# The gate of the input embedding by seven products of blocks, five of them mixed with the first row tiles of the up projection

## The chip, the cores and the metric

One core of one Trainium2 chip runs the whole layer. Its engines are TensorE (PE, matmuls, with weight loads listed as PEld), VectorE (DVE), ScalarE (ACT), GpSimd (POOL) and SyncE (SP, which issues most DMAs). The metric is the device time of one execution in microseconds (us), lower is better.

## The reference, cut to what matters

A decoder layer over 512 tokens of width 1024 in float32. The part that matters here stands between the two layer norms; h, p, w_pe and w_pe_gate have the shapes 512x1024, 512x256, 256x1024 and 1024x1024, and the up projection is 1024 wide in and 2 x 2816 wide out.

```python
h = _layer_norm(DN_ALPHA * h + mixed @ w_o[i], ln1_g[i], ln1_b[i]).astype(dt)
up = _causal_dwconv(h @ w_up[i], conv_w[i], conv_b[i])
val, gate = up[..., :D_FF], up[..., D_FF:]
ffn = (jax.nn.silu(gate) * val) @ w_down[i]
ple = (p[i].astype(dt) @ w_pe[i]) * jax.nn.sigmoid(h @ w_pe_gate[i])
h = _layer_norm(DN_ALPHA * h + ffn + ple, ln2_g[i], ln2_b[i]).astype(dt)
```

## The kernel before

Every float32 product is made of three products of rounded parts: an operand is split into a high part (ACT, a cast) and a low part (DVE, a subtraction), and `mm3` (L274) adds high x high, high x low and low x high. A matmul has a weight tile of 128x128 and 512 columns. Weights come in pages of 128x1024: `Weights` loads a page on SP's queue (L104) and splits it (L121, L122), some pages ahead of their use.

Pages are tiles of 4 KB a partition out of one pool; a page that is freed goes to the end of the list (`Pages`, L45), and its next user waits for its last reader. When the state-space part is through, `more_pages` (L1451) adds 14.

`mid` (L1103) does, in this order: the output projection of row tiles 0 and 1 (four banks, 8 k); their norms; the same for tiles 2 and 3, in which the transposes of tiles 0 and 1 are written behind k = 3 and k = 5 (`trans`, L1132: 8 transposes on PE, then 8 splits of 128x128 from PSUM into the pages hT); the norms of tiles 2 and 3; the embedding p @ w_pe of each tile (`pe`, L1121); then the gate of each tile (`gate`, L1145: 2 halves x 8 k x 3 matmuls, a sigmoid, a multiplication with the embedding, and ALPHA x row + product), with the transposes of tiles 2 and 3 behind the gates of 0 and 1. A norm is two statistics and an aggregate on DVE, 9 steps of one column on POOL for the root (`rsqrt`, L1045), and two wide steps on DVE (L1030, L1031).

`ffn_up` (L1201) follows. For each of 22 feature tiles f and each half (value, gate) it runs 24 matmuls over hT, then the convolution: one step on ACT (L1215) and two on DVE (L1216, L1217); a Silu, and for f under 16 `combine` (L1234), which makes the operands of the down projection. For that one, `Products` (L172) already takes seven products of blocks in place of eight: its pages are loaded, negated on ACT (L208) and added to another block by an accumulating DMA that POOL issues (L209). From f = 16 on these products alternate with the up projection.

The framework orders the instructions of each engine by its own simulation of their readiness. Only where `in_order` is set (L264) does each matmul stay behind the one written before it: in the attention stage and from f = 16 on, but not in `mid`.

Of the kernel before, what the change touches and what calls it, by code (L numbers as in the profile page):

```python
# [30 lines left out]
NPAGES_LATE = 14  # L31
# [140 lines left out]
class Products:  # L172
# [5 lines left out]
    ORDER = (("11", None, 0),  # L178
             ("22", None, "12"),
             ("-T3", 1, "11"),  # L180
             ("T2", 2, "21"),
             ("11", 0, "12"),
             ("21", None, 0),
             ("22", None, 0))
    KEPT = (0, 1, 2)

    def __init__(self, tc, pages, blocks, fetch_ahead=5, split_ahead=1):
        self.nc, self.pages, self.blocks = tc.nc, pages, blocks
        self.fa, self.sa = fetch_ahead, split_ahead
        self.per = NS // 2  # L190
        self.raw, self.hl = {}, {}
        self.nf = self.ns = 0
        self.n = len(self.ORDER) * self.per

# [3 lines left out]
    def fetch_to(self, n):  # L198
        while self.nf < min(n, self.n):
            q, j = divmod(self.nf, self.per)  # L200
            name, of, plus = self.ORDER[q]
            if of is None:
# [7 lines left out]
            self.raw[q, j] = pg  # L210
            self.nf += 1

    def split_to(self, n):
        while self.ns < min(n, self.n):
            self.fetch_to(self.ns + 1)
            q, j = divmod(self.ns, self.per)
            raw = self.raw[q, j]
# [4 lines left out]
            if q not in self.KEPT:  # L222
                self.raw.pop((q, j)).free()
# [8 lines left out]
    def free(self, n):  # L232
        for pg in self.hl.pop(n):
            pg.free()


class Layer:
    def __init__(self, tc, cst, pages, banks, a):
# [16 lines left out]
        self.wpg = add("w_pe_gate")  # L255
# [3 lines left out]
        self.WP = Products(tc, pages, a["w_down_blocks"])  # L259


    def mm(self, out, lhsT, rhs, start, stop):
        ins = self.nc.tensor.matmul(out=out, lhsT=lhsT, rhs=rhs, start=start, stop=stop, skip_group_check=True).ins  # L263
        if self.in_order:  # L264

# [837 lines left out]
    def mid(self):  # L1103
        nc, W = self.nc, self.W
        ple = []
# [15 lines left out]
        def pe(t):  # L1121
            ws = [W.use(self.wpe + k) for k in range(2)]
            pg = self.pages.get(f"ple{t}")
            for h in range(2):
# [3 lines left out]
                nc.scalar.copy(pg.t[:, h * 512:h * 512 + 512], bank.t)  # L1128
                bank.free()
            ple.append(pg)  # L1130
# [411 lines left out]
```

## Time and profile before

| | us |
|---|---|
| median of three runs | 794.27 |
| these runs | 796.55, 791.86, 794.27 |
| the profiled execution | 791.56 |
| its span, first to last instruction | 789.9 |
| PE busy in it | 774.6 |
| DVE busy | 546.0 |
| ACT busy | 365.9 |

The span is a little under the time of the execution it belongs to. Busy time of an engine is the time in which at least one of its instructions runs, so overlapping matmuls count once. The stage of `mid` is the stretch from 330.9 to 432.5 us; the up projection begins there and ends among the down products near 716.

### The profile page before, as it was taken

How to read it: one execution, taken by the hardware profiler on the slowest of the kernel's cores; microseconds unless marked ns; L12 is line 12 of the kernel's file. 1: busy time of each engine (PE TensorE's matmuls, PEld its weight loads, DVE VectorE, ACT ScalarE, POOL GpSimd, SP SyncE). 2: the span in 40 equal slices, each digit the busy share in tenths (PEclk: the TensorE clock that was granted, in tenths of full speed). 3: DMA queues.
4: the chain of work that ended last, by engine and by line, in shares of the span. 5: the costliest groups of instructions: out<-in, count | busy, mean ns of one | idle time of the engine just before them, and what ended most of it. 6: DMA issues, size and time to landing. Idle time of an engine off the chain costs nothing.

```text
span 789.9 us, 9826 instructions
## 1 busy us (share of the span) xinstructions
PE 774.6 (98%) x3668; PEld 647.7 (82%) x3668; DVE 546.0 (69%) x960; ACT 365.9 (46%) x578; POOL 34.7 (4%) x74
## 2 busy tenths in 40 slices
PE   9999999999999999999999999999999999999996
PEld 7888888878888888888888888888888878888885
DVE  6967998697666968947753675665755576778456
ACT  6435667664343356514522344343444676556300
POOL 0000000000000000005300000000001211000000
PEclk9999999999999999999999999999999999999998
DMA  8913221024112547515212352013325986428102
GB/s 315 391 72 101 60 74 61 27 85 132 51 54 69 182 151 293 168 46 172 96 54 79 108 191 77 0 54 107 134 100 116 256 194 137 104 84 278 39 27 81
DMA packets 32176, 95.14 MB, mean 120 GB/s; under 512 B 4480, under 2 KB 8704, under 8 KB 31872
## 3 DMA queue, kind: packets, MB, share of 16 engines
q1 hardware_dynamic: 29248, 85.07, 31.7%
q0 software_dynamic: 2304, 8.39, 5.8%
q10 hardware_dynamic: 576, 1.05, 0.4%
q8 instruction: 29, 0.48, 0.2%
q14 instruction: 19, 0.16, 0.1%
HBM read 88.20 MB, written 3.15 MB: 116 GB/s over the span
## 4 chain that ended last, share of the span: by engine, by line
PE 90%; DVE 3%; ACT 2%; DMA 2%; issue 1%; SPq 0%; DVEq 0%; ACTq 0%
PE up L263 28%; PE g L263 10%; PE o L263 6%; PE pg L263 6%; PE mx L263 6%; PE X L263 5%; PE z L263 4%; PE Y L263 4%; PE V L263 4%; PE u L263 3%; PE A L263 3%; PE v L263 3%; PE kb L263 2%; PE qb L263 2%; DMA dr<-in_w_down_blocks_dram 2%; PE pe L263 1%
## 5 line engine op out<-in xcount | busy, mean ns | idle before, releaser
L263 PE MATMUL up<-hT,wh 128*128 128x512 f32 x704 | 216.7, 389 | 0.0
L122 DVE TENSOR_TENSOR wl<-wr,wh 128x1024 fp32r<-128x1024 f32 (+1 forms) x113 | 136.1, 1213 | 65.3 <-ACT wh L121 58.3
L121 ACT CAST wh<-wr 128x1024 fp32r<-128x1024 f32 (+1 forms) x113 | 116.9, 1041 | 100.1 <-PE up L263 17.7
L263 PEld LDWEIGHTS up<-hT,wh 128*128 128x128 f32 x704 | 132.2, 188 | 27.2
L263 PE MATMUL up<-hT,wl 128*128 128x512 f32 x352 | 137.1, 390 | 0.9 <-DVE wl L122 0.9
L293 DVE SCALAR_TENSOR_TENSOR cv<-up,cw,cv 128x511 f32<-128x511 f32 x88 | 65.8, 748 | 44.1 <-ACT cv L1215 42.9
L263 PE MATMUL g<-xs,wh 128*128 128x512 f32 x256 | 81.1, 398 | 0.0
L263 PEld LDWEIGHTS up<-hT,wl 128*128 128x128 f32 x352 | 66.1, 188 | 15.1 <-DVE wl L122 1.4
L1215 ACT ACTIVATE cv<-up,cb,cw 128x512 f32<-128x512 f32 x44 | 34.1, 776 | 60.1 <-PE up L263 60.1
L263 PEld LDWEIGHTS g<-xs,wh 128*128 128x128 f32 x256 | 46.2, 188 | 8.6 <-issue 0.6
L263 PE MATMUL g<-xs,wl 128*128 128x512 f32 x128 | 50.1, 391 | 0.0
L221 DVE TENSOR_TENSOR dl<-dr,dh 128x1024 fp32r<-128x1024 f32 x28 | 34.1, 1222 | 9.7 <-ACT dh L220 8.9
L263 PE MATMUL pg<-wh,hT 128*128 128x512 f32 x128 | 40.3, 391 | 0.0
L263 PE MATMUL o<-wh,mx 128*128 128x512 f32 x128 | 39.9, 391 | 0.0
L263 PE MATMUL mx<-yts,wh 128*128 128x512 f32 x128 | 39.3, 389 | 0.0
L220 ACT CAST dh<-dr 128x1024 fp32r<-128x1024 f32 x28 | 29.3, 1046 | 8.1 <-DMA dr<-in_w_down_blocks_dram 3.1
L263 PE MATMUL X<-dh,slS 128*128 128x512 f32 x96 | 30.4, 389 | 0.0
L263 PEld LDWEIGHTS g<-xs,wl 128*128 128x128 f32 x128 | 24.0, 188 | 5.4
L263 PEld LDWEIGHTS mx<-yts,wh 128*128 128x128 f32 x128 | 24.0, 188 | 5.0
L263 PEld LDWEIGHTS pg<-wh,hT 128*128 128x128 f32 x128 | 24.0, 188 | 4.9
L263 PEld LDWEIGHTS o<-wh,mx 128*128 128x128 f32 x128 | 24.0, 188 | 4.9
L263 PE MATMUL z<-sp,tri 128*128 128x128 f32 (+3 forms) x160 | 27.2, 301 | 0.0
(229 smaller groups left out, 1382.7 us busy)
## 6 DMA issues: line engine op xcount, KB each, us to landing
wr<-in_w_up_dram SPq DMA_DIRECT2D x44, 512.0 KB, 3.4
wr<-in_w_g_dram SPq DMA_DIRECT2D x16, 512.0 KB, 3.4
dr<-in_w_down_blocks_dram SPq DMA_DIRECT2D x16, 512.0 KB, 4.2
dr<-in_w_down_blocks_dram POOLq DMA_DIRECT2D x16, 512.0 KB, 6.6
wr<-in_w_qk_dram SPq DMA_DIRECT2D x8, 512.0 KB, 10.5
wr<-in_w_glu_dram SPq DMA_DIRECT2D x8, 512.0 KB, 5.8
wr<-in_w_o_dram SPq DMA_DIRECT2D x8, 512.0 KB, 4.3
wr<-in_w_pe_gate_dram SPq DMA_DIRECT2D x8, 512.0 KB, 3.7
```

The costliest lines, as they stand in the source:

```text
L121: self.nc.scalar.copy(hi.t[:, c], raw.t[:, c])
L122: self.nc.vector.tensor_tensor(out=lo.t[:, c], in0=raw.t[:, c], in1=hi.t[:, c].bitcast(F32), op=ALU.subtract)
L220: self.nc.scalar.copy(hi.t, raw.t)
L221: self.nc.vector.tensor_tensor(out=lo.t, in0=raw.t, in1=hi.t.bitcast(F32), op=ALU.subtract)
L263: ins = self.nc.tensor.matmul(out=out, lhsT=lhsT, rhs=rhs, start=start, stop=stop, skip_group_check=True).ins
L293: self.nc.vector.scalar_tensor_tensor(out=out, in0=a, scalar=s, in1=b, op0=op0, op1=op1)
L1215: nc.scalar.activation(y, bank.t, AF.Identity, scale=cw[:, 2:3], bias=cb)
```

## The change

With h cut into two by two blocks (256 rows x 512 columns) and w_pe_gate into two by two blocks of 512x512, the gate's four blocks are sums of seven products of sums of blocks (the scheme that the down projection already uses, with another order and other sums). `mid` makes products 0 and 1 behind the output projection, then the embedding with the transposes of tiles 2 and 3, and then gives way: `run` starts the up projection and lets `mid` go on by two steps at each yield of it, so that products 2 to 6 alternate with its first five halves of a feature tile. From product 0 to the end of `mid` the matmuls (and the transposes) stay in the order in which they are written. The transposed rows are copied whole to rT (float32, needed for the sums of blocks) and split from there by two tiles at a time into two fixed tiles that replace the eight pages hT. The pool gets 6 pages instead of 14. The first three Silus become a sigmoid and a multiplication.

The core of the diff (`order`, `kept` and `per` of `Products` become parameters or follow from them; lines that only carry these through are left out):

```diff
+    GATE = (("11", None),
+            ("21", None),
+            ("22", "12"),
+            ((0, 2), None),
+            ("11", "12"),
+            (3, "21"),
+            ("22", None))
...
+            of, plus = self.order[q]
+            if isinstance(of, str):
                 pg = self.pages.get(f"dr{self.nf}")
-                self.nc.sync.dma_start(pg.t, self.block(name, j))
-            else:
+                self.nc.sync.dma_start(pg.t, self.block(of, j))
+            elif isinstance(of, int):
+                if self.ns <= of * self.per + j:
+                    return
                 pg = self.raw.pop((of, j))
             if plus:
                 self.nc.scalar.mul(pg.t, pg.t, -1.0)
                 self.nc.gpsimd.dma_start(pg.t, self.block(plus, j), accum_op=ALU.add)
-            self.raw[q, j] = pg
+            if not isinstance(of, tuple):
+                self.raw[q, j] = pg
...
+            of = self.order[q][0]
+            if isinstance(of, tuple):
+                x, y = (self.raw.pop((i, j)) for i in of)
+                self.nc.vector.tensor_tensor(out=y.t, in0=x.t, in1=y.t, op=ALU.subtract)
+                x.free()
+                self.raw[q, j] = y
...
+        self.WG = Products(tc, pages, a["w_pe_gate_blocks"], Products.GATE, fetch_ahead=6, split_ahead=2)
...
         def trans(t):
-            r = self.res[t].t
+            r, h = self.res[t].t, t // 2
             for b in range(2):
+                if t % 2 == 0:
+                    rT[h, b] = self.pages.get(f"rT{h}{b}", F32, (P, 4, 2 * P))
                 bank = self.banks.get(f"ht{t}{b}", (P, 4, P))
                 for kk in range(4):
                     k = 4 * b + kk
-                    nc.tensor.transpose(bank.t[:, kk], r[:, k * P:k * P + P], self.ident)
-                for kk in range(4):
-                    k = 4 * b + kk
-                    o = slice(t * P, t * P + P)
-                    self.split(self.hT[k].t[:, 0, o], self.hT[k].t[:, 1, o], bank.t[:, kk])
+                    self.ordered(nc.tensor.transpose(bank.t[:, kk], r[:, k * P:k * P + P], self.ident).ins)
+                nc.scalar.copy(rT[h, b].t[:, :, t % 2 * P:t % 2 * P + P], bank.t)
                 bank.free()
-
-        def gate(t):
-            ws = [W.use(self.wpg + k) for k in range(KT)]
-            tp = self.pages.get(f"plg{t}")
-            for h in range(2):
-                hs = slice(h * 512, h * 512 + 512)
-                bank = self.banks.get(f"pg{t}{h}")
-                for k in range(KT):
-                    self.token_mms(bank, self.hT[k], t, h, ws[k], k, k == 0, k == KT - 1)
-                self.actf(2, tp.t[:, hs], bank.t, AF.Sigmoid)
-                bank.free()
-            self.tt(tp.t, tp.t, ple[t].t, ALU.mult)
-            r = self.res[t].t
-            self.stt(r, r, ALPHA, tp.t, ALU.mult, ALU.add)
-            tp.free()
-            ple[t].free()
+                if t % 2 == 1:
+                    o = slice(256 * h, 256 * h + 256)
+                    self.split(big[b][:, :, 0, o], big[b][:, :, 1, o], rT[h, b].t)
+        def split_sum(name, src):
+            pg = [self.pages.get(f"{name}{x}", F32R, (P, 4, 2 * P)) for x in range(2)]
+            self.split(pg[0].t, pg[1].t, src)
+            return pg
+        def block(h, c, src):
+            if isinstance(src, list):
+                pg = self.pages.get(f"plg{h}{c}", F32, (P, 2, T))
+                for m in range(2):
+                    self.actf(2, pg.t[:, m], src[m].t, AF.Sigmoid)
+            else:
+                pg = src
+                self.actf(2, pg.t, pg.t, AF.Sigmoid)
+            self.tt(pg.t, pg.t, ple[h, c].t, ALU.mult)
+            ple[h, c].free()
+            for m in range(2):
+                r = self.res[2 * h + m].t[:, 512 * c:512 * c + 512]
+                self.stt(r, r, ALPHA, pg.t[:, m], ALU.mult, ALU.add)
+            pg.free()
+        def saved(name, bank):
+            pg = self.pages.get(name, F32, (P, 2, T))
+            for m in range(2):
+                nc.scalar.copy(pg.t[:, m], bank[m].t)
+            return pg
+        def plus(pg, bank):
+            for m in range(2):
+                self.tt(pg.t[:, m], pg.t[:, m], bank[m].t, ALU.add)
+            return pg
+        def product(q, bank, a, fresh=False):
+            if fresh:
+                bank.extend(self.banks.get(f"pg{q}{m}") for m in range(2))
+            for j in range(2):
+                n = 2 * q + j
+                hi, lo = (pg.t.rearrange("p (k n) -> p k n", k=2) for pg in WG.use(n))
+                for m in range(2):
+                    ts_ = slice(m * P, m * P + P)
+                    for k in range(2):
+                        kk = 2 * j + k
+                        self.mm3(bank[m].t, a(kk, 0, ts_), a(kk, 1, ts_), hi[:, k], lo[:, k],
+                                 fresh and kk == 0, kk == 3)
+                WG.free(n)
+                yield
+        def of_block(h, b):
+            return lambda k, x, s: big[b][:, k, x, 256 * h + s.start:256 * h + s.stop]
+        def of_sum(pg):
+            return lambda k, x, s: pg[x].t[:, k, s]
...
-            if k >= 2:
+            if 2 <= k < 4:
                 W.use(self.wpe + k - 2)
+            if k >= 4:
+                WG.split_to(k - 5)
+                WG.fetch_to(k - 1)
             if k == 3:
-                self.hT = [self.pages.get(f"hT{k}", F32R, (P, 2, T)) for k in range(KT)]
                 trans(0)
             if k == 5:
                 trans(1)
         norm(3)
         self.g1.free()
         self.b1.free()
+        self.in_order, self.last_mm = True, None
+        ple = {(h, c): self.pages.get(f"ple{h}{c}", F32, (P, 2, T)) for h in range(2) for c in range(2)}
+        X, Y, V = [], [], []
+        yield from product(0, X, of_block(0, 0), True)
+        x1 = saved("gx", X)
+        yield from product(1, V, of_block(0, 1), True)
+        plus(x1, V)
+        drop(*V)
         for t in range(4):
             pe(t)
+            if t < 2:
+                trans(t + 2)
             yield
+        block(0, 0, x1)
         for k in range(2):
             W.free(self.wpe + k)
             self.pT[k].free()
-        for t in range(4):
-            gate(t)
-            if t < 2:
-                trans(t + 2)
-            yield
-        for k in range(KT):
-            W.free(self.wpg + k)
+        a11, a12, a21, a22 = (rT[h, b].t for h in range(2) for b in range(2))
+        self.tt(a21, a21, a11, ALU.subtract)
+        s3 = split_sum("s3", a21)
+        self.tt(a22, a21, a22, ALU.add)
+        rT[1, 0].free()
+        self.up_ready = True
         yield
+        yield from product(2, Y, of_sum(s3), True)
+        drop(*s3)
+        s2 = split_sum("s2", a22)
+        y7 = saved("gy", Y)
+        yield from product(3, X, of_sum(s2))
+        drop(*s2)
+        self.tt(a11, a22, a11, ALU.add)
+        s1 = split_sum("s1", a11)
+        rT[0, 0].free()
+        u2 = saved("gu", X)
+        yield from product(4, X, of_sum(s1))
+        drop(*s1)
+        plus(y7, X)
+        self.tt(a12, a12, a22, ALU.subtract)
+        rT[1, 1].free()
+        s4 = split_sum("s4", a12)
+        rT[0, 1].free()
+        yield from product(5, Y, of_block(1, 1))
+        block(1, 1, y7)
+        plus(u2, Y)
+        drop(*Y)
+        yield from product(6, X, of_sum(s4))
+        drop(*s4)
+        block(1, 0, u2)
+        block(0, 1, X)
+        drop(*X)
+        self.in_order = False
...
-            self.actf(3, yp.t[:, 1], yp.t[:, 1], AF.Silu)
+            if f < 3:
+                sg = self.pages.get(f"sg{f}", F32, (P, T))
+                self.actf(2, sg.t, yp.t[:, 1], AF.Sigmoid)
+                self.tt(yp.t[:, 1], yp.t[:, 1], sg.t, ALU.mult)
+                sg.free()
+            else:
+                self.actf(3, yp.t[:, 1], yp.t[:, 1], AF.Silu)
...
+        self.up_ready = False
+        mid = self.mid()
+        while not self.up_ready:
+            next(mid)
         products, acc = None, 0.0
         for f in self.ffn_up():
+            for _ in range(2):
+                next(mid, None)
...
+        late = ctx.enter_context(tc.tile_pool(name="late", bufs=1))
+        lay.hT_tiles = [late.tile([P, 4, 2, T], F32R, name=f"hT{q}") for q in range(2)]
+        lay.pages.more(late, NPAGES_LATE)
```

## Rows read from the trace of the kernel before

**Rows 1.** PE's waits, whole span: line, releaser, us in total, times, longest.

```profile
PE z L263 <- ACT wp L300: 1.8, 2, 1.6
...
PE up L263 <- DVE wl L122: 0.9, 1, 0.9
```

**Rows 2.** Windows: length, busy PE, PEld, DVE, ACT, POOL, clock, DMA, GB/s.

```profile
376.20:432.50 56.30, 56.30 (x258) 46.69 (x257) 30.57 (x49) 19.64 (x41) 6.69 (x18) 1.00 0.19 62
432.50:606.80 174.30, 174.30 (x770) 144.43 (x769) 109.04 (x160) 70.61 (x88) 1.84 (x2) 1.00 0.30 98
606.80:635.00 28.20, 27.40 (x121) 22.36 (x120) 14.66 (x19) 18.21 (x21) 6.10 (x8) 1.00 0.99 247
```

**Rows 3.** The chain that ended last, from 320 to 440: start, us, what.

```profile
370.71 5.49 PE o L263 x24
...
381.70 1.39 PE pg L263 x6
383.08 5.44 PE pe L263 x24
...
398.05 0.87 PE ht L1138 x8
...
410.69 21.77 PE pg L263 x96
```

**Rows 4.** Groups of DVE and ACT, 287 to 476: count, busy, mean ns, idle.

```profile
L122 DVE TENSOR_TENSOR wl<-wr,wh 128x1024 fp32r<-128x1024 f32 x33 | 39.8, 1222 | 17.0 <-ACT wh L121 16.7
L281 DVE TENSOR_TENSOR hT<-ht,hT 128x128 fp32r<-128x128 f32 x32 | 7.9, 284 | 0.7
L284 DVE TENSOR_TENSOR mt<-mt,gate 128x512 f32<-128x512 f32 x8 | 5.5, 690 | 0.0
...
L293 DVE SCALAR_TENSOR_TENSOR cv<-up,cw,cv 128x510 f32<-128x510 f32 x7 | 5.2, 748 | 0.2
...
L284 DVE TENSOR_TENSOR se<-cv,se 128x256 f32<-128x256 f32 x2 | 0.9, 426 | 0.1
...
L121 ACT CAST wh<-wr 128x1024 fp32r<-128x1024 f32 x33 | 34.5, 1050 | 38.7 <-PE o L263 15.1 <-DMA wr<-in_w_glu_dram 8.2 <-DMA wr<-in_w_pe_gate_dram 5.4
...
L1128 ACT COPY ple<-pe 128x512 f32<-128x512 f32 x8 | 4.5, 591 | 4.1 <-PE pe L263 4.1
```

**Rows 5.** DMA issues, 350 to 440, then 600 to 720; last: us to landing.

```profile
wr<-in_w_up_dram SPq DMA_DIRECT2D x11, 512.0 KB, 3.4
...
dr<-in_w_down_blocks_dram POOLq DMA_DIRECT2D x15, 512.0 KB, 6.7
```

**Rows 6.** DVE in order of time: start, us, instruction, idle before it.

```profile
378.15 1.22 DVE L122 TENSOR_TENSOR wl<-wr,wh 128x1024 fp32r<-128x1024 f32 x1
...
380.88 0.69 DVE L1018 BATCH_NORM_STATS2 ln_st<-x 128x6 f32<-128x512 f32 x1
381.48 0.67 DVE L293 SCALAR_TENSOR_TENSOR x<-x,o 128x512 f32<-128x512 f32 x1
...
384.05 0.33 DVE L1028 BATCH_NORM_AGGREGATE ln_mv<-ln_st 128x2 f32<-128x12 f32 x2
...
391.20 2.48 DVE L293 SCALAR_TENSOR_TENSOR x<-x,ln_rs,b 128x1024 f32<-128x1024 f32 x2 [4.44 <-POOL ln_rs L1058]
```

**Rows 7.** POOL in order of time, from 352 to 436.

```profile
358.27 1.24 POOL L1058 TENSOR_SCALAR ln_rs<-ln_rs,ln_ri 128x1 f32<-128x1 f32 x1
...
386.91 0.22 POOL L1052 TENSOR_SCALAR ln_rs<-ln_rs 128x1 f32<-128x1 f32 x1
...
390.92 0.49 POOL L1058 TENSOR_SCALAR ln_rs<-ln_rs 128x1 f32<-128x1 f32 x2
```

**Rows 8.** Windows with a crowded DVE; the last has products among up halves.

```profile
152.00:172.00 20.00, 18.12 (x100) 15.59 (x98) 18.06 (x40) 13.18 (x28) 0.00 (x0) 1.00 0.18 61
309.00:330.90 21.90, 21.90 (x98) 18.15 (x97) 20.74 (x28) 12.03 (x18) 0.00 (x0) 1.00 0.41 133
635.00:716.00 81.00, 80.87 (x357) 66.99 (x358) 59.37 (x74) 49.73 (x64) 6.04 (x7) 1.00 0.54 133
```

More of the change, by code (lines that the diff above doesn't have):

```diff
@@ L30 @@
 NPAGES, NHALVES = 37, 6
-NPAGES_LATE = 14
+NPAGES_LATE = 6
 NS = 8
@@ L172, with __init__ @@
 class Products:
[L178 to L188, printed above, removed]
+    DOWN = (("11", None),
+            ("22", "12"),
+            (1, "11"),
+            (2, "21"),
+            (0, "12"),
+            ("21", None),
+            ("22", None))
+    GATE = (("11", None),
+            ("21", None),
+            ("22", "12"),
+            ((0, 2), None),
+            ("11", "12"),
+            (3, "21"),
+            ("22", None))
+    def __init__(self, tc, pages, blocks, order, fetch_ahead=5, split_ahead=1):
+        self.nc, self.pages, self.blocks, self.order = tc.nc, pages, blocks, order
         self.fa, self.sa = fetch_ahead, split_ahead
-        self.per = NS // 2
+        self.per = blocks.shape[2]
         self.raw, self.hl = {}, {}
         self.nf = self.ns = 0
-        self.n = len(self.ORDER) * self.per
+        self.n = len(order) * self.per
+        self.kept = {x for of, _ in order if not isinstance(of, str) for x in (of if isinstance(of, tuple) else [of])}
     def block(self, name, j):
@@ L234, in free, with __init__ @@
             pg.free()
+class View:
+    def __init__(self, t):
+        self.t = t
 class Layer:
@@ L254, in __init__ @@
         self.wpe = add("w_pe")
-        self.wpg = add("w_pe_gate")
         self.wup = add("w_up")
@@ L1103, in mid @@
     def mid(self):
-        nc, W = self.nc, self.W
-        ple = []
+        nc, W, WG, rT = self.nc, self.W, self.WG, {}
+        big = self.hT_tiles
+        self.hT = [View(big[k // 4][:, k % 4]) for k in range(KT)]
         def out_mms(k, ts):
@@ L1162, in mid, with drop @@
+        def of_block(h, b):
+            return lambda k, x, s: big[b][:, k, x, 256 * h + s.start:256 * h + s.stop]
+        def of_sum(pg):
+            return lambda k, x, s: pg[x].t[:, k, s]
+        def drop(*pages):
+            for pg in pages:
+                pg.free()
         bk = {(t, h): self.banks.get(f"o{t}{h}") for t in range(2) for h in range(2)}
@@ L1230, in ffn_up @@
             yield f
-        for pg in self.hT:
-            pg.free()
     def combine(self, f, yp):
@@ L1453, in more_pages @@
         ssm_pool.close()
-        lay.pages.more(ctx.enter_context(tc.tile_pool(name="late", bufs=1)), NPAGES_LATE)
+        late = ctx.enter_context(tc.tile_pool(name="late", bufs=1))
+        lay.hT_tiles = [late.tile([P, 4, 2, T], F32R, name=f"hT{q}") for q in range(2)]
+        lay.pages.more(late, NPAGES_LATE)
     lay.more_pages = more_pages
@@ L1502, in layouts @@
         "w_pe": _rows(i["w_pe"][0], 1),
-        "w_pe_gate": _rows(i["w_pe_gate"][0], 1),
+        "w_pe_gate_blocks": i["w_pe_gate"][0].reshape(2, 2, 2, P, 2, 512).transpose(0, 4, 1, 3, 2, 5)
+        .reshape(2, 2, 2, P, 1024),
         "w_up": up,
```

14 lines of the change are left out of this document (5 added, 9 removed).

## The prediction

> **What bounds the kernel now.** I read the view of PE's waits first: over the whole span it names nine, 7.3 us together, 5.1 of them in the attention stage; the longest is for wp there, and the only one behind the attention is 0.9 us [rows 1]. Then the windows by stage: in the one that holds the gate (376.2 to 432.5) and in the up projection behind it PE is busy to the last hundredth, DVE for 54% and 63%, ACT for less [rows 2]. So where the change works, a matmul taken away is worth its full price, and every microsecond in which PE waits for a new operand is paid in full.
>
> **What is taken away.** The gate is 4 row tiles x 2 halves x 8 k x 3 = 192 matmuls. The chain of waits shows the price: the 96 of tiles 2 and 3 run in one piece of 21.77 us [rows 3], 0.2268 us each. Seven products of 2 row tiles x 4 k x 3 make 168. So 24 go, 24 x 0.2268 = 5.44 us, which is the whole of the gain. Transposes, products with w_pe and the up projection keep their matmuls.
>
> **What is added beside PE.** By 1.22 us for a DVE step of 128x1024 and 0.69 for one of 128x512, 1.05 and 0.59 on ACT [rows 4]: six more weight pages to split (14 for 8), four sums and four splits of activations, two differences of weight pages: 16 wide DVE steps, 19.5 us. Six additions from PSUM (x1, y7, u2) and three multiplications by a sigmoid: 9 x 0.69 = 6.2. The 32 small splits of hT (0.284 each, 9.1 us) become four wide ones, 4.9. DVE gets +21.5 us. ACT gets ten splits (10.5), six negations (6.4) and six copies (3.5): +20.4; its 32 small steps turn into 8 copies and 4 wide splits (8.9). The multiplications with the embedding and the sigmoids of the gate are cut otherwise and sum to about the same. The sigmoids in place of the first three Silus leave one change of ACT's table, as now. On the DMA side 8 loads become ten on SP's queue and six that accumulate on POOL's, +4.2 MB; a load lands after 3.4 us and an accumulating one after 6.7 [rows 5]. The first of these chains (load, negate, accumulate, split) is started some 10 us ahead of its product, the later ones 20: 3.4 + 1.06 + 6.7 + 2.3 = 13.5 us. The first could be late by 3, but it feeds the third product, due 29 us after the second half of the output projection ends; so the two products ahead of it hide it and I put it at nothing; without them PE would wait for it by those 3 us.
>
> **The new PE order, and where it can wait.** From the first product on the order is written out, so PE can no longer fill a hole with other matmuls, as it does now: 6 of pg go ahead of 24 of pe [rows 3]. With PE full from 376.2, where the output projection ends [rows 3]: two products (10.88), pe of tile 0 (2.72), so the transpose of row tile 2 is due at 389.8; then 0.87, pe 2.72, tile 3 at 393.4, done 394.3; two pe's; the first half of the up projection at 399.7; then products 2 to 6 and up halves in turn, the last product at 394.3 + 10 x 5.44 = 448.7.
>
> First place: *the transpose of tile 2*. It needs its norm. Now both aggregates stand at 384.4 [rows 6], POOL's Newton steps end at 391.4 [rows 7], and DVE's last steps of the two tiles, from 391.2 on, end near 392.4 and 393.7 [rows 6]. Nobody waits, since the transpose comes at 398.05 [rows 3]. In the new order that would be 392.4 - 389.8 = 2.6 us late. In its favour: from 376 to 384 DVE now also does eight small hT splits and two wl; the new splits of tiles 0 and 1 are two wide ones that can be done by 376. With eight steps of 0.6 us from start to start [rows 6] the aggregates could stand at 381.4, with two weight splits between at 383.8; the 7.0 us of POOL (384.4 to 391.4) and 1.2 of DVE make 389.6 to 392.0: 0 to 2.2 late, and I take the middle, 1.1. Upper bound: the two chains share POOL with the issue of up to three accumulating loads, each as long as a blocked step, 1.24 [rows 7]: 2.2 + 3.7 = 5.9. Tile 3 then comes 3.6 us behind tile 2 on PE and 1.3 on DVE, and is covered.
>
> Second place: *DVE from 394.3 to 448.7*. In these 54.4 us it has to do 27 wide steps (2 splits of hT, 8 weight splits of gate, 5 of up, 4 sums, 4 splits, 2 differences, 2 in the merges), 10 of 512, 8 convolution steps of 0.75 and 9 of 256: 32.9 + 6.9 + 6.0 + 3.8 = 49.6, 91%. Nearest rows [rows 8]: in 309 to 331 DVE is at 95% and PE loses nothing; in 635 to 716 (down products and up halves in turn, order written out, DVE 73%) PE loses 0.13 of 81; in 152 to 172 (90%) 1.88 of 20. The bounds for 54.4 us are 0 and 9.4% = 5.1. The lossy row is attention, where PE waits for wp [rows 1], the end of a chain over three engines; the new stage has the splits of the other two. So I take 0.3, near those.
>
> Smaller ones: the first product needs hT of tiles 0 and 1; the transposes end at 370.7 and two copies, two splits and a subtraction (1.2 + 2.1 + 1.2 us) end at 375.2, before 376.2: 0, at most 1. Eight pages of the pool become fixed for hT: before, they came back only when the up projection was through, so what the down products share is as large as before; 0, from -0.9 (the last wait of [rows 1] gone) to +1.
>
> **Sum.** 791.56 us is the profiled execution (its span is 789.9); 791.56 - 5.44 + 1.1 + 0.3 = 787.5, that is -4.0. The median of the runs, 794.27, lies 2.7 above that execution; so the forecast is 794.27 - 4.0 = 790.3.
>
> **Rivals.**
> *All is hidden* (waits under 1 us): 794.27 - 5.44 = 788.8. For it: no loss at all in 376 to 606 now [rows 2], and DVE at 95% without loss in 309 to 331. Against it: 389.8 is ahead of 392.4.
>
> *The norm chain is late.* POOL's one-column steps take 0.22 to 0.25 us where DVE is idle and up to 1.24 where DVE runs without a gap [rows 7]. If the new weight splits keep DVE full while the 18 steps run, the norms come later: the 5.9 of above and the 5.1 of a crowded DVE behind it give up to 794.27 - 5.44 + 11.0 = 799.8; likelier a wait of 3 to 7, near 794. [...]
>
> *Slower: the operands of products 3 and 4 come behind the convolution.* s2 and s1 are written in the code behind an up half. If ACT and DVE take them in that order, each begins when that half's last matmul is done: 3 x 0.75 (convolution) + 0.6 (sigmoid) + 1.05 + 1.22 = about 5.1 us of idle PE, twice 10.2. With the 1.4 of the forecast: 794.27 - 5.44 + 11.6 = 800.4. It turns slower from 9.4 us of waits (5.44 + 0.5%), that is when both are late. Against it: the scheduler orders by readiness, as the pg matmuls ahead of pe show, and a weight split that stands among norm steps [rows 3, 6].
>
> *Nothing left over.* The 28 us from 606.8 on run with DMA at 0.99, and PE there has no slack (the 0.9 us) [rows 1, 2]. If other pages make one accumulating load late by its own 6.7 us there, 794.27 - 4.0 + 6.7 = 797.0.
>
> **How the numbers follow.** Forecast (waits 1 to 3 us) 0.34, all hidden 0.28, norm chain 0.15, late operands 0.14, nothing left 0.09. A measurement of this kernel can tell about 0.5% (4.0 us) from no change, so faster needs waits under 1.5: all hidden and half of the forecast, 0.45; slower is the late operands, 0.14; the rest is the same, 0.41. The range reaches from the fastest run, 791.86, less 5.44 (786.4) into the norm chain's upper part (waits of 9 us); it leaves out the late operands and the last of the norm chain: 786 to 798.
>
> **What would show it.** Right: 168 matmuls on the new products at 0.227 us, PE waiting 1 to 2 us ahead of the transpose of tile 2 for DVE's last norm step, DVE near 90% from there to the last product, and about 5.4 us less between 376 and the fourth pair of up halves, less the waits. Wrong: waits ahead of products 3 and 4 for split steps; a transpose of tile 2 later than 393; new waits behind 600; or waits on loads that are negated and accumulated.

## The result, and the profile after

| | before | after |
|---|---|---|
| median of 22 runs each, us | 793.56 (791.11 to 797.42) | 798.79 (792.21 to 802.78) |
| ratio of the runs, 95% interval | 1 | 1.0054 (1.0036 to 1.0072) |
| the profiled execution, us | 791.56 | 800.49 |
| its span | 789.9 | 798.8 |

The changed kernel is slower by half a per cent (4.3 us by the ratio, 5.2 by the medians); 790.3 was forecast. The runs of before lie in two groups of about equal size, 791 to 793 and 794 to 797, and only 3 of the 22 of after lie below 795; why one kernel has both groups is not settled here.

The page of after, engine totals and then a DMA queue (packets, MB, share): 24 matmuls and 24 weight loads fewer than the 3668 of before, PE's busy time only 0.9 us shorter.

```profile
PE 773.7 (97%) x3644; PEld 646.1 (81%) x3644; DVE 567.8 (71%) x961; ACT 386.1 (48%) x577; POOL 41.7 (5%) x80
...
q8 instruction: 28, 0.46, 0.2%
```

PE's waits of after, whole span, as [rows 1]:

```profile
PE up L287 <- DVE wl L122: 6.6, 1, 6.6
PE ht L1167 <- DVE x L320: 3.2, 1, 3.2
PE z L287 <- ACT wp L327: 2.0, 3, 1.6
```

Two waits are new. The 3.2 us stand where they were foretold, ahead of the transpose of tile 2. The 6.6 us stand at the end of the mixed stretch of the down projection, where before had 0.9. Together they are 9.8 us, against a gain of 5.44.

The chain of after from 390 to 412, against [rows 3]:

```profile
390.02 1.32 POOL ln_rs L1084
...
392.85 1.30 DVE x L320
394.14 0.04 issue
394.19 1.97 PE ht L1167 x8
396.16 3.19 PE pe L287 x12
399.34 0.87 PE ht L1167 x8
400.22 5.49 PE pe L287 x24
405.70 5.44 PE up L287 x24
```

It runs through POOL's steps of the norm's root, DVE's last norm step and the transpose. Eight transposes take 1.97 us at first and 0.87 at the second tile; 12 matmuls of pe take 3.19, where 24 take 5.49. The windows of after (columns as in [rows 2]) say why:

```profile
377.00:405.00 28.00, 24.76 (x112) 20.52 (x111) 23.32 (x29) 17.72 (x24) 14.61 (x22) 0.94 0.58 117
391.00:394.20 3.20, 0.01 (x1) 0.01 (x1) 2.08 (x4) 2.40 (x4) 2.73 (x7) 0.89 0.00 0
394.20:396.20 2.00, 2.00 (x9) 2.00 (x10) 1.07 (x1) 0.86 (x2) 1.71 (x3) 0.50 0.00 0
405.70:454.70 49.00, 49.00 (x218) 40.57 (x217) 36.92 (x44) 24.78 (x30) 0.00 (x0) 1.00 0.31 101
606.00:650.00 44.00, 37.24 (x154) 30.01 (x153) 20.65 (x27) 23.33 (x27) 8.60 (x10) 0.92 0.83 193
```

Behind the wait the granted clock is 0.50 from 394.2 to 396.2, so the stage lost 3.2 us of waiting and (1.97 - 0.87) + (3.19 - 5.49/2) = 1.5 us of slow matmuls: 4.7 of the 5.44. From 405.7 to 454.7, where products 2 to 6 alternate with up halves, PE loses nothing, with DVE at 36.92/49 = 75%. The last row is the stretch of the second wait.

### The profile page after: what moved, and what is told of

Its sections match the earlier page's. It is cut to its first block, busy times and chain, and to the rows that moved or that the text cites. A ratio compares the mean times of both kernels' runs of the same rounds, so it can differ in the third digit from the quotient of the medians.

```text
span 798.8 us, 9816 instructions
## 1 busy us (share of the span) xinstructions
PE 773.7 (97%) x3644; PEld 646.1 (81%) x3644; DVE 567.8 (71%) x961; ACT 386.1 (48%) x577; POOL 41.7 (5%) x80
## 3 DMA queue, kind: packets, MB, share of 16 engines
q10 hardware_dynamic: 576, 1.05, 0.4%
## 4 chain that ended last, share of the span: by engine, by line
PE 88%; DVE 4%; ACT 3%; DMA 2%; issue 1%; POOL 1%; DVEq 0%; SPq 0%; ACTq 0%
PE up L287 29%; PE g L287 11%; PE X L287 5%; PE mx L287 5%; PE o L287 5%; PE z L287 4%; PE Y L287 4%; PE V L287 4%; PE pg L287 3%; PE u L287 3%; PE A L287 3%; PE v L287 3%; PE kb L287 2%; PE qb L287 2%; DMA dr<-in_w_down_blocks_dram 1%
## 5 line engine op out<-in xcount | busy, mean ns | idle before, releaser
L122 DVE TENSOR_TENSOR wl<-wr,wh 128x1024 fp32r<-128x1024 f32 (+1 forms) x105 | 126.6, 1212 | 57.3 <-ACT wh L121 47.0
L121 ACT CAST wh<-wr 128x1024 fp32r<-128x1024 f32 (+1 forms) x105 | 108.7, 1042 | 84.5 <-DMA wr<-in_w_up_dram 14.9
L237 ACT CAST dh<-dr 128x1024 fp32r<-128x1024 f32 x42 | 43.7, 1046 | 31.0 <-DMA dr<-in_w_pe_gate_blocks_dram 13.4
L238 DVE TENSOR_TENSOR dl<-dr,dh 128x1024 fp32r<-128x1024 f32 x42 | 50.9, 1221 | 8.6 <-ACT dh L237 7.6
L218 ACT ACTIVATE dr<-dr 128x1024 f32<-128x1024 f32 x22 | 23.3, 1059 | 26.1 <-DMA dr<-in_w_down_blocks_dram 13.8
L219 POOL DMA_DIRECT2D dr<-in_w_down_blocks_dram x16 | 13.8, 861 | 270.1 <-ACT dr L218 270.1
```

The lines of the kernel that those rows point to most:

```text
L121: self.nc.scalar.copy(hi.t[:, c], raw.t[:, c])
L122: self.nc.vector.tensor_tensor(out=lo.t[:, c], in0=raw.t[:, c], in1=hi.t[:, c].bitcast(F32), op=ALU.subtract)
L218: self.nc.scalar.mul(pg.t, pg.t, -1.0)
L219: self.nc.gpsimd.dma_start(pg.t, self.block(plus, j), accum_op=ALU.add)
L237: self.nc.scalar.copy(hi.t, raw.t)
L238: self.nc.vector.tensor_tensor(out=lo.t, in0=raw.t, in1=hi.t.bitcast(F32), op=ALU.subtract)
```

## The norm chain: where the 3.2 us come from

DVE of after in order of time (as [rows 6]), then POOL (as [rows 7]):

```profile
378.13 1.22 DVE L238 TENSOR_TENSOR dl<-dr,dh 128x1024 fp32r<-128x1024 f32 x1
...
381.65 1.21 DVE L238 TENSOR_TENSOR dl<-dr,dh 128x1024 fp32r<-128x1024 f32 x1
382.78 1.22 DVE L231 TENSOR_TENSOR dr<-dr,dr 128x1024 f32<-128x1024 f32 x1
...
384.52 0.19 DVE L1055 BATCH_NORM_AGGREGATE ln_mv<-ln_st 128x2 f32<-128x12 f32 x1
384.62 1.17 DVE L122 TENSOR_TENSOR wl<-wr,wh 128x1024 fp32r<-128x1024 f32 x1
385.71 1.22 DVE L231 TENSOR_TENSOR dr<-dr,dr 128x1024 f32<-128x1024 f32 x1
...
392.85 1.29 DVE L320 SCALAR_TENSOR_TENSOR x<-x,ln_rs,b 128x1024 f32<-128x1024 f32 x1 [1.12 <-POOL ln_rs L1085]
```

```profile
384.80 1.07 POOL L1078 TENSOR_SCALAR ln_rs<-ln_mv 128x1 f32<-128x1 f32 x1 [1.87 <-DVE ln_mv L1055]
385.95 1.05 POOL L1079 TENSOR_SCALAR ln_rs<-ln_rs 128x1 f32<-128x1 f32 x1
387.06 1.18 POOL L1080 TENSOR_SCALAR ln_ri<-ln_rs 128x1 int32<-128x1 int32 x1
388.35 1.20 POOL L1084 TENSOR_SCALAR ln_rs<-ln_ri,ln_rs 128x1 f32<-128x1 f32 x1
389.65 0.27 POOL L1085 TENSOR_SCALAR ln_rs<-ln_rs,ln_ri 128x1 f32<-128x1 f32 x1
390.02 1.32 POOL L1084 TENSOR_SCALAR ln_rs<-ln_rs 128x1 f32<-128x1 f32 x1
```

Among the norm's steps DVE runs weight work that is due much later: two splits of L238 (by their order the pages of product 2, which PE reaches at 411), a split of the up projection (reached at 405.7) and both differences of L231, which make the weights of product 3, a product that PE reaches only near 422. So the first aggregate is done at 384.7 and the second at 387.0. Then each of five POOL steps lasts about as long as the wide DVE step beside it (1.05 to 1.32 us beside 1.17 to 1.28, against 0.22 to 0.34 for others), where before, with DVE idle from 386.8 to 391.2, a step takes 0.19 to 0.33 (its shortest group in [rows 7] 0.22). The root of tile 2 alone ends at 392.8, 8.1 us behind its aggregate; before, POOL made both tiles' roots in 7.0.

## The down projection: where the 6.6 us come from

SP's order of loads is the same in both kernels, and at 606 us after is only 0.44 us behind. SP and ACT of before, then of after (start, us; in brackets the idle time ahead and its releaser); the first row of each is the issue of one pair of plain loads, the others are the negations that ACT makes when a load has landed:

```profile
606.35 0.80 SPq L204 DMA_DIRECT2D dr<-in_w_down_blocks_dram  x2
...
610.43 1.06 ACT L208 ACTIVATE dr<-dr 128x1024 f32<-128x1024 f32 x1 [3.07 <-DMA dr<-in_w_down_blocks_dram]
...
614.26 1.06 ACT L208 ACTIVATE dr<-dr 128x1024 f32<-128x1024 f32 x1 [2.24 <-DMA dr<-in_w_down_blocks_dram]
...
625.05 1.06 ACT L208 ACTIVATE dr<-dr 128x1024 f32<-128x1024 f32 x1 [0.68 <-DMA dr<-in_w_down_blocks_dram]
```

```profile
606.79 1.61 SPq L212 DMA_DIRECT2D dr<-in_w_down_blocks_dram  x2
...
615.02 1.06 ACT L218 ACTIVATE dr<-dr 128x1024 f32<-128x1024 f32 x1 [7.22 <-DMA dr<-in_w_down_blocks_dram]
...
616.51 1.04 ACT L218 ACTIVATE dr<-dr 128x1024 f32<-128x1024 f32 x1
...
631.61 1.06 ACT L218 ACTIVATE dr<-dr 128x1024 f32<-128x1024 f32 x1 [2.78 <-DMA dr<-in_w_down_blocks_dram]
```

Issuing the pair takes 1.61 us in place of 0.80. Of before one load lands by 610.4 and the other by 614.3; of after ACT gets the first only at 615.0. What has moved 4.2 us behind the issue says how the first load is late (before from 606.35 to 610.55, then after from 606.79 to 610.99; packets of all queues, then q1, the queue of the plain loads):

```profile
DMA packets 187, 0.70 MB, mean 167 GB/s; under 512 B 16, under 2 KB 16, under 8 KB 187
...
q1 hardware_dynamic: 144, 0.52, 50.9%
```

```profile
DMA packets 178, 0.68 MB, mean 162 GB/s; under 512 B 15, under 2 KB 15, under 8 KB 177
...
q1 hardware_dynamic: 137, 0.50, 47.3%
```

144 packets are one load: 128 of 4 KB and 16 small ones. After lacks 7 of them, one of the small ones among them. So nearly all of the load is on time, and its last few packets are not. ACT is idle for 7.22 us ahead of the negation at 615.02; a convolution and the next negation come behind it, and so do the accumulating loads that need the negations. One pair later the same negation comes at 631.61 in place of 625.05, 6.56 us late, and ACT's next weight casts with it: that is the 6.6.

What differs at 606 is a transfer that no line of the kernel issues. DMA by queue (packets, MB, share) of before from 600 to 606, and of after from 606 to 612; in tenths of a microsecond it starts between 600.9 and 601.0 in before, and between 606.8 and 606.9 in after:

```profile
q8 instruction: 1, 0.02, 1.3%
```

```profile
q8 instruction: 1, 0.02, 1.2%
```

The queue's name and its bytes suggest that it carries PE's program: after has 2 x 3644 = 7288 instructions on PE, and 0.46 MB / 7288 = 63 bytes each; before 0.48 MB for 7336, 65 each. That it does is my reading, and by the queue's name its transfers are called code transfers here. As an estimate from these numbers, one of the 28 of after, 16 KB (0.46 MB / 28), comes for some 260 instructions or 130 matmuls, at 0.227 us each about 29 us. 24 matmuls fewer would shift each later transfer by 24/130 of that, 5.4 us, against the work around it: from some 5.4 us ahead of the pair of loads (600.9 and 606.35 in before) onto its issue (606.8 and 606.79 in after). The other instruction queue of the page, q14, does not go with the lateness: after and the run after_12_more below, of which only the first has the late pair, both have a transfer of it some 2 us ahead of the pair. That q8's transfer is the cause was so far a theory; the last experiments put it to the test.

## The experiments

Each ratio is against runs of before on the same chip (medians 792.03 to 793.61). The runs lie on several chips, so two experiments are compared by their ratios as well as by their medians; a difference of 0.2% between them is within their intervals. Three rivals were open at first: the wait at the transpose is all of it; the gate's accumulating loads or the mixed order cost the rest; or the loss stands in the down projection and has another cause.

**late_transposes.** The transposes of tiles 2 and 3 go behind three of the four pe.

```diff
             pe(t)
-            if t < 2:
-                trans(t + 2)
...
+            if t == 3:
+                trans(2)
+                trans(3)
+            pe(t)
```

> The changed kernel with one edit: the transposes of row tiles 2 and 3 stand behind the third embedding product (pe of tile 2) instead of behind the first and the second; DVE's, ACT's and POOL's order is the same. Theory 1 (the written-out order makes PE wait for the norm of tile 2: 3.2 us, and PE runs slower for the next 20 matmuls, 1.6 us): the transposes are due 5.4 us later, the wait goes, and the kernel is 3 to 4.8 us faster than the changed one. Rival 1a (the wait only moves to the first up half, which then waits for hT of tiles 2 and 3): a wait ahead of the up projection of 2 to 4 us, no gain. The wait in the down products' first stretch, 6.6 us in the changed kernel's profile, should stay under both.

Measured 790.4, ratio 0.9968 (0.9945 to 0.9991). The gain did not come from the transposes: in its profiled execution (794.74) the wait there is 1.6 and two waits of the first up half for hT are 0.8 and 0.7, and PE is busy for 24.92 us of 377 to 405, after 24.76; it saves the slow clock at most. The code transfer starts between 604.0 and 604.1, just ahead of a pair issued at 604.31 in 1.18 us. That pair is not late: its first load lands after 4.2 us, as in before. The execution still has a wait of 4.5 us for wl, from the next pair, whose first load takes 7.5 us to land in place of 5.7, with no code transfer near. The median is 4.3 below this execution; why the others don't have that wait, and where the transfer lies in them, can't be read, since one alone has a profile. So this run, with after's number of matmuls, is not slow, and its transfer lies ahead of the issue.

**after_plain_down, before_plain_down.** The 16 accumulating loads of the down products and their negations are left out, in either kernel, so the down projection computes with the plain blocks.

```diff
-            if plus:
+            if plus and self.accumulate:
```

> The changed kernel with the down products' sixteen accumulating loads and their sixteen negations on ACT left out (the loads from SP stay, so the down products are taken with unmixed blocks); the gate is as changed. Theory 2 (most of the loss of the change against the forecast arises in the stretch from 606 us on, where a plain load lands late behind accumulating ones and PE waits 6.6 us and then runs slower): without them PE has no wait there, and this kernel is 6 to 9 us faster than the changed one. Against the old kernel with the same edit it should then be between 1.5 us faster and 0.5 slower, that is -5.44 of matmuls and +4 to +5 of the norm wait. Rival 2a (the loss is in the gate's stage or spread over all): the pair keeps the difference of 4 to 5 us that the full kernels have.

> The old kernel with the down products' sixteen accumulating loads and negations left out, the same as in the changed one. Theory 2: its stretch from 606 us on has no wait of PE; it is 1 to 4 us faster than the old kernel, whose runs lie in two groups, near 791.7 and near 796. Rival 2a: as fast as the old kernel less the 0.9 us of the wait in its profile, with two groups still.

Measured 790.16, 0.9968 (0.9944 to 0.9992), and 790.12, 0.9972 (0.9952 to 0.9993). With the down chain out of the way the two kernels are equal: the gate as changed is worth nothing, its gain used up by the norm wait (still 3.2 in the profile of the first). All of the slowdown belongs to the down projection. In the first of them the code transfer lies on the pair again (between 608.1 and 608.2, the pair issued at 608.04 in 1.42 us), and the two loads land after 4.6 us in the median, in place of 3.7 in the second: without accumulating loads beside it the same coincidence goes with 0.9 us, which PE doesn't wait for.

**after_early_loads, before_early_loads.** The pair of loads is asked for sooner, by one line in the up projection's loop; it is then issued as two single loads, at 587.6 and 594.1 in the first kernel.

```diff
             if f == 2 * NS - 1:
                 self.WP.split_to(1)
+                self.WP.fetch_to(self.WP.nf + 1)
```

> The changed kernel with one edit: the fifth and sixth load of the down products (the first two that are negated) are asked for half a feature tile to one feature tile earlier, while f = 15 is written instead of f = 16. Theory 2 (the pair of loads that is issued at 606.8, right behind an accumulating load, lands after 8 us and holds up ACT's queue and then PE): the pair is issued before that accumulating load, PE's wait behind 606 falls from 6.6 us to under 1, and the kernel is 4 to 8 us faster than the changed one. Rival 2b (the DMA engines are full there anyway, and another load takes the place of the pair): PE waits as long, somewhat later, no gain.

> The old kernel with the same edit as after_early_loads: the fifth and sixth load of the down products are asked for earlier. Theory 2 (in this kernel too the slower half of the runs, near 795, is that late load; the gate of the change is worth nothing by itself): one group of runs, 789 to 791, 0.3 to 0.6% under the old kernel and within 0.2% of after_early_loads (789.4). Rival 2c (the early loads help only the changed kernel): no difference to the old kernel, so that the changed gate, with them, is worth the 0.5% by which after_early_loads was faster.

Measured 789.43, 0.9952 (0.9928 to 0.9977), and 789.74, 0.9967 (0.9946 to 0.9988). No wait is left behind 606 in either. By the medians the line takes 9.4 us from after and 3.8 from before; the difference, 5.6, is the slowdown of 5.2. The two kernels are again equal within 0.3 us, so what follows on the gate is measured on this base.

**root_on_dve.** After with the early loads, and the root's one-column steps on DVE in place of POOL.

```diff
-        eng = self.nc.gpsimd
+        eng = self.nc.vector
```

> The kernel after_early_loads with the nine one-column steps of each first norm's root on DVE in place of POOL. Theory 3 (PE's wait ahead of the transpose of tile 2, 3.2 us in the changed kernel's profile, is POOL's chain: 7.9 us from the aggregate at 384.7 to the last step at 392.8, four of its steps at 1.05 to 1.32 us because they wait for DVE steps): the chain shrinks to some 2 to 4 us, the transpose has its row at about 389, PE's wait falls to under 1 us, and the kernel is 3 to 5 us faster than after_early_loads, near 785. Rival 3a (DVE is what is full: eighteen more steps there push the statistics and the splits back): the wait stays at 2 to 4 us, or the first products wait for their weights.

Measured 792.25, 0.9982 (0.996 to 1.0003): slower than its base. A step takes 0.14 us there, but the steps stand in a queue full of weight work, with splits and differences between them, and the wait is longer than in its base (4.1 in two waits, the longest 3.2):

```profile
PE ht L1167 <- DVE x L320: 5.3, 1, 5.3
```

So taking the root off POOL gains nothing while DVE's queue stays as it is.

**unmixed_early.** Early loads, and all seven products ahead of the up projection, the Silus kept.

```diff
-        while not self.up_ready:
-            next(mid)
+        for _ in mid:
+            pass
```

> The kernel after_early_loads with all seven products ahead of the up projection, as `mid` writes them, with no up halves between (and the first three Silus as Silus). Theory 4 (the mixing is what hides the DVE work of products 2 to 6): these five products are 27.2 us of PE, for 24 wide DVE steps less those of the up halves, about 19 x 1.22 + 8 x 0.69 = 29 us, with each sum, split and product behind the last: PE waits for operands or weights between the products, 5 to 15 us in sum, and the kernel is that much slower than after_early_loads, 794 to 804. Rival 4a (the operands are ready in time anyway): within 1 us of after_early_loads.

Measured 790.73, 0.9966 (0.9944 to 0.9988), 1.3 above its base, with intervals that overlap: the mixed order costs nothing and is worth about 1 us at most. Part of the reason is in its chain: `in_order` binds only matmuls that are made while it is set, and at 409.7 the scheduler by itself puts up matmuls among those of pg.

**late_early.** Early loads and the later transposes.

> The kernel after_early_loads with the transposes of tiles 2 and 3 behind the third embedding product, as in late_transposes. Theory 1 (the wait ahead of the transpose of tile 2 is what makes the changed gate worth nothing): with the down products' stretch quiet, the gain is that of the wait, 2 to 4 us against after_early_loads, near 786. Rival 1a (the wait moves ahead of the first up half; in late_transposes PE lost 3.1 us in 377 to 405, 3.2 in the changed kernel, and what that run gained it gained in the down products): no gain, 789.

Measured 788.84, 0.9938 (0.9915 to 0.996), 0.6 better than its base: the wait mostly moves, from the transposes (1.6) to the up half behind them (0.8 + 0.7), 3.1 in all for 4.1 in the base.

**norm_first.** Early loads, and on DVE the splits of the gate's fifth and later weight pages and the two differences are ordered behind the last norm step of tile 3.

```diff
+        WG.behind = lambda ins, n: self.after(ins, self.norm_last) if n >= 4 else None
```

> The kernel after_early_loads with one more edit: on DVE the split of the gate's fifth weight page and all DVE steps of later pages (the two differences for product 3 among them) are ordered behind the last step of tile 3's norm. Theory 5 (PE's wait ahead of the transpose of tile 2 is DVE's queue: between the end of the output projection and the aggregates it runs 3 wide weight steps, then 3 more beside POOL's chain, each of which holds a POOL step for 1.05 to 1.3 us; root_on_dve did not help since that queue stayed): the aggregates stand at about 382, POOL's 18 steps run at 0.2 to 0.35 us, the row of tile 2 is ready near 388 to 390, PE's wait falls from 3.2 to under 1 us, no PE steps at the lower clock follow it, and the kernel is 3 to 5 us faster than after_early_loads, near 785. Rival 5a (the work held back is then late for products 2 and 3, or for the first up half): a wait of 2 to 4 us behind 394 in its place, no gain.

Measured 790.79, 0.9974 (0.9952 to 0.9996): no gain yet. The wait at the transpose is gone, but pe waits 2.2 for gx and pg 1.1 for s. POOL in order of time shows what is late now:

```profile
384.78 0.86 POOL L220 DMA_DIRECT2D dr<-in_w_pe_gate_blocks_dram  x1 [1.84 <-ACT dr L219]
385.71 2.10 POOL L1079 TENSOR_SCALAR ln_rs<-ln_mv 128x1 f32<-128x1 f32 x2
```

This profiled execution (795.04) is 4.3 above the median and later than that of after throughout, so times are best counted from the start of product 0, at 379.99 here and 377.19 in after. Both aggregates are done by 384.2, 4.3 us behind it (after: 7.5 and 9.9), but the root stands behind the issue of an accumulating load, which waits for its negation, and its first two steps take 1.05 us each, as long as those beside a wide DVE step in after. The chain ends at 392.4, 12.4 us behind that start, both tiles together (after: 15.6 for tile 2 alone).

**norm_first_root.** The same, and the root on DVE.

> The kernel norm_first with the root's nine one-column steps on DVE in place of POOL. Theory 5: with DVE's queue free of the weight steps the chain on DVE is 18 steps of 0.06 to 0.12 us, but one of the additions to x1 stands among them and waits for product 1 (387); the row of tile 2 is ready at about 390: as fast as norm_first within 1 us. If POOL's chain is what is left in norm_first (its wait still over 1 us), this one is faster by that wait.

Measured **785.65** in seven runs (784.94 to 789.08), 0.9913 (0.9884 to 0.9943): faster than both kernels, and 4.1 of the 5.44 below before with the early loads. The window that lost 3.2 us of PE in after, and DVE's last norm steps:

```profile
377.00:405.00 28.00, 28.00 (x133) 23.12 (x131) 27.22 (x47) 19.09 (x28) 2.57 (x3) 1.00 0.39 95
```

```profile
387.59 2.48 DVE L1059 SCALAR_TENSOR_TENSOR x<-x,ln_rs,b 128x1024 f32<-128x1024 f32 x2
```

The norms are ready at 390.1 in place of 394.1 and 398.8 (14.5 us behind the start of product 0 in place of 17.0 and 21.6), and PE is full; 0.9 us of waiting for s is left at 406. Either edit alone gains nothing, both together do: DVE's queue has to be free of later work, and the root off a queue that waits for other things.

**gate_plain.** After with the gate's six accumulating loads and their negations left out.

```diff
-            if plus:
+            if plus and not self.plain:
```

> The changed kernel (late loads of the down products as it has them) with the gate's six accumulating loads and their negations left out, so that the gate is taken with unmixed weight blocks; the down products keep their sixteen. Theory 6 (the six accumulating loads ahead of them are why the down products' loads land late in nearly all runs of the changed kernel and in half of the old one's): the slow group of runs, 797 to 802, shrinks to half of them or fewer, median near 792. Rival 6a (it is the place in time of the whole stretch, or chance): the runs stay near 798, less up to 1 us for the ACT and POOL work that is gone from the norm's stretch.

Measured 799.84, 1.0077 (1.0052 to 1.0102), with the same waits of 6.6 and 3.2. Leaving out the gate's accumulating loads gains nothing. It has after's number of matmuls, and its code transfer starts between 606.1 and 606.2, inside the issue of a pair from 605.62 to 607.46.

**after_12_more, before_52_more.** Matmuls of 8 x 8 are added to the warm-up at the start of the kernel, 12 to after and 52 to before; each shows as two matmuls in the trace (24 and 104). They do nothing for the result; they are to move q8's transfers against the work. The 24 give after the 3668 matmuls of before; by the estimate above the 104 move the transfers of before by 104/130 x 29 = 23 us, so that the one behind that of 601 should lie at about 601 + 29 - 23 + 2.5 (the time of the matmuls) = 609.5.

```diff
             self.mm(bank.t[:, 0:P], pg.t, pg.t, True, True)
+        for _ in range(12):
+            self.mm(bank.t[0:8, 0:8], pg.t[:, 0:8], pg.t[:, 0:8], True, True)
```

> The changed kernel with twelve more matmuls of 8x8 in the warm-up at its start (each is two matmul instructions and two weight loads, as the nine there are), which use nothing and are used by nothing. PE's program is then as long up to the down products as the old one's, within a few instructions; a transfer of program code of 16 KB (queue q8 of the profile) that the changed kernel has at 606.5 us, in the very half microsecond of the pair of loads at 606.8, moves back to about 6 us ahead of that pair, where the old kernel has it (600.5). Theory 7 (that coincidence delays the second load of the pair and is why the changed kernel nearly always has the slow stretch): the pair is issued within 0.8 us as in the old kernel instead of 1.6, and half of the runs or more lie below 794; median 1 us or so (the warm-up's length) above where the gate alone would put it, 792 to 795. Rival 7a (code transfers don't matter): the runs stay near 798 to 800.

> The old kernel with fifty-two more matmuls of 8x8 in the warm-up, so that its code transfer falls where the changed kernel has it, on the pair of loads at 606. The start grows by at most some 5 us, which the profile shows as the start of the first projection. Theory 7: beside that growth the runs move into the slow group: median 4 to 7 us above 791.5 plus the growth, and the pair is issued 1.2 to 1.8 us long. Rival 7a: the runs stay in two halves, at 791.5 and 796 plus the growth.

Measured 791.71 (789.93 to 796.69), 0.9996 (0.9973 to 1.0019): more work on PE, and 7.1 us less than after (4.6 by the ratios). And 801.57 in six runs (795.12 to 804.02), 1.0101 (1.0063 to 1.0139): 9.5 more than before (8.0 by the ratio), of which the matmuls themselves account for 2.5 (PE's first matmul of u starts at 7.93 us in place of 5.48). SP and ACT, as above, of the first and then the second; of the second also PE's wait:

```profile
606.30 0.81 SPq L212 DMA_DIRECT2D dr<-in_w_down_blocks_dram  x2
...
610.35 1.06 ACT L218 ACTIVATE dr<-dr 128x1024 f32<-128x1024 f32 x1 [3.03 <-DMA dr<-in_w_down_blocks_dram]
```

```profile
607.91 1.45 SPq L204 DMA_DIRECT2D dr<-in_w_down_blocks_dram  x2
...
614.90 1.06 ACT L208 ACTIVATE dr<-dr 128x1024 f32<-128x1024 f32 x1 [5.98 <-DMA dr<-in_w_down_blocks_dram]
```

```profile
PE up L263 <- DVE wl L122: 6.6, 1, 6.6
```

In the changed kernel the last transfers lie near 544, 572 and 601, as in before (after: 550, 578, 607), and the pair is issued and lands as in before. In the old kernel, with no edit of the gate, one starts between 607.9 and 608.0, on the pair, and the long issue, the late landing and the 6.6 us are all there. The profiled execution of after_12_more (796.03) still has a wait of 3.9 for wl, and is 4.3 above its median. As in late_transposes it comes from the next pair (issue 1.16 us, the first load landing after 7.1), with no code transfer between 601 and 632: so a load was late there without a code transfer too, and what made it late isn't settled.

## Why the prediction was wrong, step by step

- *What bounds the kernel; the price of a matmul.* Right: 24 matmuls of a product take 5.44 us in the chain, 168 in place of 192.
- *What is added beside PE.* Right: DVE has 21.8 us more (forecast 21.5), ACT 20.2 (20.4), the DMAs 4.2 MB. What failed is where this work stands.
- *The stretch of the products (0.3, up to 5.1).* Right, and less: no loss from 405.7 to 454.7. DVE is at 75% there and not 91%, since some of its weight steps ran ahead of 394, in the norm's way.
- *The rival of late operands at products 3 and 4 (800.4).* It did not occur; the measured time lies near its number by another cause.
- *The first product, and the loads that are negated and accumulated.* No PE wait there, and gate_plain shows nothing gained without them.
- *The transpose of tile 2 (1.1, up to 5.9).* The place was right and the term mis-sized: 3.2 of waiting and 1.5 of slow matmuls, 4.7. Two steps failed. One is "the aggregates could stand at 381.4, with two weight splits between at 383.8", of which the middle was taken. In its favour stood "eight small hT splits" that DVE no longer has to do; the trace of before has five of them between 376 and 384. And three weight splits and two differences stood among the norm steps: the first aggregate came at 384.7, or at 383.6 without the 1.15 us by which the profiled execution was behind when product 0 began, so at the late end, and the second at 387.0. The other is the 8.2 us from the aggregates to the row ("the 7.0 us of POOL" and 1.2 of DVE): with a wide DVE step beside five of its nine steps, tile 2's row took 9.4. I took the scheduler's readiness for an order by need; these steps were ready because their loads were started early. The granted clock behind a wait had no term at all. The rival of the norm chain, with its "up to 1.24" for a POOL step, was near: in after five POOL steps of one column took 1.05 to 1.32 us beside DVE steps of 1.17 to 1.28. Their length alone is not what cost the time: root_on_dve, where a step took 0.14 us, was slower than its base (792.25 for 789.43).
- *Smaller ones: the down projection (0, from -0.9 to +1), and the rival "nothing left over" (6.7).* This step decided the sign: the term that was put at 0 came out at +5.2 to +5.5 us (the slowdown less the 0.0 and -0.3 us that the pairs of plain_down and early_loads leave to the gate). That PE has no slack there and that one late load costs 6.7 us was read rightly: 6.6 of wait. But I looked for a cause among pages and gave it 0.09. The cause is the position of q8's transfer, which the change in the number of matmuls ahead of 606 moved, by 5.4 us as estimated and from 601 to 606.8 as measured. The trace of before showed the queue and its transfers.
- *The sum.* -5.44 + 4.7 in the gate is -0.7, and the profiled execution has it (0.44 us behind before at 606, of which 1.18 were lost ahead of 332); by medians the two pairs give 0.0 and -0.3. The 5.2 of the slowdown are the down projection's. The base of 794.27 was the median of three runs and is 793.56 with 22. 798.79 is outside of the range (786 to 798).

## What to carry to other kernels

A step that is ready isn't a step that is needed: when a change puts early-loaded work on an engine that also carries a short chain with a deadline, order that work behind the chain, and look at every queue on which the chain stands (here both edits were needed, 785.65 us). Where a stretch has its DMAs at 0.99 and no slack on PE, look at what the kernel doesn't issue as well: here the queue named instruction moved 16 KB about every 29 us, and with 24 matmuls fewer its transfer of 601 came at 606.8. Compare such a change with and without the fragile stretch in both kernels, before its own stage is blamed or praised.

## What the runs showed of the hardware

- A code transfer of 16 KB inside the issue of a pair of 512 KB loads goes with an issue of 1.42 to 1.84 us (after_plain_down 1.42, before_52_more 1.45, after 1.61, gate_plain 1.84) in place of 0.80 in before and 0.81 in after_12_more, and of 1.18 us where it starts just ahead (late_transposes). With accumulating loads in flight the pair's first load then lands after 7.0 to 8.4 us (after, gate_plain, before_52_more) in place of 4.0 to 4.2 (before, after_12_more, late_transposes), and what is late in after are the last 7 of its 144 packets; without accumulating loads the pair lands after 4.6 us (after_plain_down) in place of 3.7 (before_plain_down). That the transfer's position is the cause is shown by 12 and 52 small matmuls, which took that lateness away (the first load landing after 4.0 us) and brought it on (7.0). How so small a transfer does this stays open.
- Behind PE's wait of 3.2 us the granted clock was 0.50 for 2 us in the profiled execution of after, and 1.00 in the same stretch of after_early_loads: the eight transposes behind the wait took 1.97 and 1.09 us. So the price of a wait in slow matmuls was not the same in these two runs.
- A one-column step of the root took 0.14 us on DVE (root_on_dve), 0.19 to 0.34 on POOL (before and after), and 1.05 to 1.32 on POOL beside a wide DVE step of 1.17 to 1.28 (after).
